# Layernorm with a residual add: the first store moved ahead of two loads in the transfer queue

## The chip, the cores and the metric

The kernel runs on one core of one Trainium2 chip. The metric is the device time of one execution in microseconds (us), the median of several. The span on a profile page is about 1.3 us shorter than that time. Engines are named as the profile names them: DVE is VectorE, ACT is ScalarE, POOL is GpSimd, and SP is SyncE, which here computes nothing and only issues transfers.

## The reference

```python
z = x + residual                      # 16 x 1024 x 512, float32
mean = np.mean(z, axis=-1, keepdims=True)
var = np.var(z, axis=-1, keepdims=True)
out = gamma * (z - mean) / np.sqrt(var + eps) + beta
```

Two inputs of 33.55 MB are read and one output of 33.55 MB is written, 100.66 MB in all. Each input byte is used once.

## The kernel before

The kernel calls 128 tokens (one per partition, 2 KiB each) a row. There are 128 rows. Sixteen rows of one tensor are 4 MiB. All large transfers are issued by SP, in the order of a written plan; `x0+8` loads rows 0 to 7 of x, `r` is the residual, `o` the store of finished rows.

```python
Z_ROWS = 64      # rows of zbuf: x comes here, is added to, normalized, and stored from here
R_ROWS = 32      # rows of rbuf: the residual

PLAN = """
x0+8 r0+8 x8+8 r8+8 x16+16 r16+16 x32+16 r32+16
x48+16 r48+16 o0+16 r64+16 x64+16 o16+16 r80+16 x80+16
o32+16 r96+16 x96+8 x104+8 o48+16 r112+16 x112+8 x120+8
o64+16 o80+16 o96+16 o112+12 o124+4
"""
ADDS = [4, 4, 8] * 7 + [4] * 4        # rows per POOL instruction
```

SP walks this plan. A wait in front of one transfer also holds everything behind it in the plan:

```python
for kind, lo, n in moves:
    if kind == "x":      # the rows of zbuf must have been stored
        while gone < len(stores) and stores[gone][0] < lo + n - Z_ROWS:
            nc.sync.wait_ge(so[gone], 16)
            gone += 1
        move(...)
    elif kind == "r":    # the rows of rbuf must have been added
        wait_rows(s_add, "add", lo + n - R_ROWS)
        move(...)
    else:                # the rows must be finished
        wait_rows(s_out, "out", lo + n)
        move(...)
```

So x48 waits for nothing, r48 waits until rows 0 to 31 are added, r64 until rows 0 to 47 are, x64 until o0 has landed, and o0 until DVE has finished rows 0 to 15. On the other engines, POOL adds r to x in zbuf (L180), ACT makes the sums over each row in groups of four rows (L202 and L212), and DVE normalizes the same groups (L240 and L252).

## Time and profile before

| | before |
|---|---|
| time, median of 3 runs | 238.39 us |
| span in the profile | 236.9 us |
| load/store queue, share of 16 engines' span | 99.2% |
| ACT, DVE, POOL busy | 78%, 75%, 60% |

These are lines of the page of the kernel before. The row DMA is the busy share of the 16 DMA engines in 40 slices of 5.9 us, in tenths; the row below it is what they moved; "q1" is the queue of all large transfers.

```profile
span 236.9 us, 1471 instructions
PE 3.7 (2%) x4; PEld 1.2 (0%) x4; DVE 177.2 (75%) x290; ACT 185.5 (78%) x545; POOL 143.0 (60%) x29
DMA  8999999999999999999999999999999999999996
GB/s 310 443 432 426 426 443 443 443 443 443 426 415 398 443 443 443 426 420 409 431 437 443 443 443 432 420 407 429 443 437 437 409 432 448 437 420 437 426 430 285
q1 hardware_dynamic: 4176, 100.67, 99.2%
```

No slice but the first and the last falls below 9, and the mean is 425 GB/s.

The timeline of SP in the kernel before, from 31 to 99 us. The columns are the start, the duration of the issue instruction, the engine and line, the operation, and out<-in. By the plan, the lines are r32, x48, r48, o0, r64, x64, o16, r80.

```profile
31.01 0.33 SPq L146 DMA_DIRECT2D rbuf<-in_residual_dram  x1
31.38 0.43 SPq L146 DMA_DIRECT2D zbuf<-in_x_dram  x1
59.41 0.33 SPq L146 DMA_DIRECT2D rbuf<-in_residual_dram  x1
59.78 0.43 SPq L146 DMA_DIRECT2D out_dram<-zbuf  x1
78.83 0.33 SPq L146 DMA_DIRECT2D rbuf<-in_residual_dram  x1
90.61 0.33 SPq L146 DMA_DIRECT2D zbuf<-in_x_dram  x1
90.98 0.43 SPq L146 DMA_DIRECT2D out_dram<-zbuf  x1
98.55 0.33 SPq L146 DMA_DIRECT2D rbuf<-in_residual_dram  x1
```

The timeline of POOL in the kernel before: the adds of rows 32 to 47, 48 to 63 and 64 to 79. In brackets is the idle time before, and what ended it.

```profile
60.98 17.83 POOL L180 TENSOR_TENSOR zbuf<-zbuf,rbuf 128x2048 f32<-128x2048 f32 x3 [1.60 <-DMA rbuf<-in_residual_dram]
80.67 17.84 POOL L180 TENSOR_TENSOR zbuf<-zbuf,rbuf 128x2048 f32<-128x2048 f32 x3 [1.87 <-DMA rbuf<-in_residual_dram]
109.81 17.85 POOL L180 TENSOR_TENSOR zbuf<-zbuf,rbuf 128x2048 f32<-128x2048 f32 x3 [11.29 <-DMA zbuf<-in_x_dram]
```

The start of an add says when its last load landed: r32 at 60.9 us, r48 at 80.7, x64 at 109.8. The transfers thus land in plan order, 4 MiB each 9.7 to 9.9 us. When SP issued r48 at 59.41 us, r32 was just ending and x48 was still to come.

### The profile page before, as it was taken

The numbers are of one execution on the slowest core, as the hardware profiler recorded it, in microseconds if no ns is written. First come the engines' busy times: TensorE is split into PE (matmuls) and PEld (weight loads), VectorE is DVE, ScalarE is ACT, GpSimd is POOL, SyncE is SP. The second block draws the span as 40 slices with busy tenths as digits, with TensorE's granted clock in tenths as the row PEclk, the third lists the DMA queues.
The fourth block names the chain that finished last, engine by engine and source line by source line (L and its number), as shares of the span: only waits on it lengthen the run. The fifth ranks groups of instructions, "written<-read, shape, count | busy, mean of one in ns | idle before, by whom it ended". The sixth has DMA issues, their size and how long they took to land.

```text
span 236.9 us, 1471 instructions
## 1 busy us (share of the span) xinstructions
PE 3.7 (2%) x4; PEld 1.2 (0%) x4; DVE 177.2 (75%) x290; ACT 185.5 (78%) x545; POOL 143.0 (60%) x29
## 2 busy tenths in 40 slices
PE   0600000000000000000000000000000000000000
PEld 0100000000000000000000000000000000000000
DVE  0001977939699999999898989896989895698920
ACT  2019879497999999999999998979998956999300
POOL 0098920999799699604995059944995049950000
DMA  8999999999999999999999999999999999999996
GB/s 310 443 432 426 426 443 443 443 443 443 426 415 398 443 443 443 426 420 409 431 437 443 443 443 432 420 407 429 443 437 437 409 432 448 437 420 437 426 430 285
DMA packets 4181, 100.68 MB, mean 425 GB/s; under 512 B 466, under 2 KB 466, under 8 KB 468
## 3 DMA queue, kind: packets, MB, share of 16 engines
q1 hardware_dynamic: 4176, 100.67, 99.2%
q14 instruction: 1, 0.01, 0.0%
q10 hardware_dynamic: 4, 0.00, 0.0%
HBM read 67.11 MB, written 33.55 MB: 425 GB/s over the span
## 4 chain that ended last, share of the span: by engine, by line
DMA 71%; POOL 9%; ACT 9%; DVE 2%; issue 2%; SPq 1%; ACTq 0%; DVEq 0%; POOLq 0%
DMA out_dram<-zbuf 49%; DMA rbuf<-in_residual_dram 16%; POOL zbuf L180 9%; DMA zbuf<-in_x_dram 6%; ACT junk_s L212 5%; ACT junk_m L202 4%; SPq L146 1%; DVE zbuf L240 1%; DVE zbuf L252 1%; ACTq L202 0%; DVEq L240 0%; ACT std L221 0%; DVE rstd L249 0%; ACTq L193 0%; POOLq L177 0%
## 5 line engine op out<-in xcount | busy, mean ns | idle before, releaser
L180 POOL TENSOR_TENSOR zbuf<-zbuf,rbuf 128x2048 f32<-128x2048 f32 (+1 forms) x25 | 142.8, 5740 | 67.6 <-DMA zbuf<-in_x_dram 40.8
L240 DVE SCALAR_TENSOR_TENSOR zbuf<-zbuf,nm,gamma_p 128x512 f32 x128 | 87.1, 743 | 46.3 <-ACT junk_s L212 46.3
L202 ACT ACTIVATE junk_m<-zbuf 128x512 f32 x128 | 74.9, 585 | 29.1 <-POOL zbuf L180 27.5
L212 ACT ACTIVATE junk_s<-zbuf,nm 128x512 f32 x128 | 88.8, 694 | 1.0
L252 DVE SCALAR_TENSOR_TENSOR zbuf<-zbuf,rstd,beta_p 128x512 f32 x128 | 87.1, 743 | 1.1
L212 ACT ACTIVATION_READ_ACCUMULATOR junk_s<-zbuf,nm 128x1 f32 x128 | 23.9, 187 | 0.0
L202 ACT ACTIVATION_READ_ACCUMULATOR junk_m<-zbuf 128x1 f32 x128 | 23.9, 187 | 0.0
L221 ACT ACTIVATE std<-ssq,eps_t 128x4 f32<-128x4 f32 x32 | 9.5, 297 | 3.0
L249 DVE RECIPROCAL rstd<-std 128x4 f32<-128x4 f32 x32 | 5.5, 170 | 0.0
L190 ACT ACT_TABLE_LOAD x1 | 1.3, 1283 | 2.7 <-PEq L60 2.7
L132 PE MATMUL gamma_p<-gb_row,ones 1*128 1x512 f32 x2 | 2.0, 1119 | 7.2 <-DMA gb_row<-in_gamma_dram 7.2
L132 PE MATMUL beta_p<-gb_row,ones 1*128 1x512 f32 x2 | 1.9, 1052 | 0.0
L127 DVE MEMSET ones<- 1x128 f32 x1 | 0.2, 165 | 2.0 <-PEq L60 2.0
L132 PEld LDWEIGHTS beta_p<-gb_row,ones 1*128 1x128 f32 x2 | 0.7, 328 | 1.0 <-issue 0.5
L132 PEld LDWEIGHTS gamma_p<-gb_row,ones 1*128 1x128 f32 x2 | 0.5, 308 | 7.1 <-issue 7.1
L288 POOL MEMSET const-float32-0.0<- 128x1 f32 x1 | 0.1, 98 | 0.2 <-issue 0.2
L288 POOL MEMSET const-bfloat16-1.0<- 128x1 bf16 x1 | 0.1, 101 | 0.0
L288 POOL MEMSET const-uint8-127<- 128x1 uint8 x1 | 0.1, 101 | 0.0
L288 POOL MEMSET const-float32-1.0<- 128x1 f32 x1 | 0.1, 98 | 0.0
L128 DVE MEMSET eps_t<- 128x1 f32 x1 | 0.1, 59 | 0.0
## 6 DMA issues: line engine op xcount, KB each, us to landing
rbuf<-in_residual_dram SPq DMA_DIRECT2D x7, 4096.0 KB, 30.5
out_dram<-zbuf SPq DMA_DIRECT2D x7, 4096.0 KB, 28.6
zbuf<-in_x_dram SPq DMA_DIRECT2D x5, 4096.0 KB, 28.9
zbuf<-in_x_dram SPq DMA_DIRECT2D x6, 2048.0 KB, 14.9
rbuf<-in_residual_dram SPq DMA_DIRECT2D x2, 2048.0 KB, 15.7
out_dram<-zbuf SPq DMA_DIRECT2D x1, 3072.0 KB, 13.5
out_dram<-zbuf SPq DMA_DIRECT2D x1, 1024.0 KB, 10.2
gb_row<-in_gamma_dram ACTq DMA_DIRECT2D x1, 2.0 KB
```

What stands on the lines that cost most here:

```text
L127: nc.vector.memset(ones[:, :], 1.0).then_inc(s_const, 1)
L132: nc.tensor.matmul(dest[:, :], ones[:, :], gb_row[:, k * D : (k + 1) * D], start=True, stop=True).then_inc(s_pe, 1)
L146: i = nc.sync.dma_start(out=out, in_=in_).then_inc(s, 16)
L180: nc.gpsimd.tensor_tensor(out=z, in0=z, in1=part(rbuf, R_ROWS, lo, n), op=ALU.add).then_inc(s_add, n)
L190: act.preload_act_table_set("sqrt_and_others")
L202: i = act.activation(out=junk_m[k][:, :], in_=zk[k], func=ACT.Identity, scale=-inv_d, accum_out=nm[j][:, k : k + 1],)
L212: i = act.activation(out=junk_s[k][:, :], in_=zk[k], func=ACT.Square, bias=nm[j][:, k : k + 1], accum_out=ssq[j][:, k : k + 1],)
L221: act.activation(out=std[j][:, :], in_=ssq[j][:, :], func=ACT.Sqrt, bias=eps_t[:, 0:1], scale=inv_d,).then_inc(s_std, TURN)
L240: dve.scalar_tensor_tensor(out=zk[k], in0=zk[k], scalar=nm[j][:, k : k + 1], in1=gamma_p[:, :], op0=ALU.add, op1=ALU.mult,)
L249: dve.reciprocal(out=rstd[j][:, :], in_=std[j][:, :]).then_inc(s_dve, TURN)
L252: i = dve.scalar_tensor_tensor(out=zk[k], in0=zk[k], scalar=rstd[j][:, k : k + 1], in1=beta_p[:, :], op0=ALU.mult, op1=ALU.add,)
L288: nc = _bacc.Bacc("TRN2", target_bir_lowering=False, num_devices=1)
```

## The change

The store of the first 16 rows is queued ahead of the two loads of the fourth 16 rows instead of behind them. The intent that the diff suggests: the store's place in zbuf comes free earlier, so that x64, which goes there, can be issued earlier.

```diff
-x48+16 r48+16 o0+16 r64+16 x64+16 o16+16 r80+16 x80+16
+o0+16 x48+16 r48+16 r64+16 x64+16 o16+16 r80+16 x80+16
```

## The prediction

> **What bounds the kernel.** The transfers. The page's queue line puts the load/store queue at 99.2% of 16 engines' span; the slice row for DMA reads 9 in every slice but the first and last; 10-us windows from 2 to 227 us show a DMA share of at least 0.95. 100.68 MB at the mean of 425 GB/s is the span, 236.9 us. The Trainium skill, "DMA: Bandwidth & Descriptors", section "Measured", has the same 425 GB/s for a 16 MB load on one core alone, so no spare rate is left. ACT has 78%, DVE 75%, POOL 60%.
>
> **What changes.** Only the SyncE queue's order: from x48, r48, o0 to o0, x48, r48. Before, the timeline shows x48 issued at 31.4 us, r48 at 59.4 (after the adds of rows 16 to 31), o0 at 59.8. Now x48 stands behind o0's wait for 16 finished rows. DVE finishes row 15 at 48.3 us, so o0 goes out then and x48 at about 48.7.
>
> **Does the queue run dry?** No. The skill's same page, "Queues, rings and completion order", says each DMA engine takes descriptors in ring order; the trace agrees (r32 lands at 60.9, r48 at 80.7, o0 at 90.6; about 9.8 us per 4 MiB). At 48.3 us the ring still holds 12.6 us of work. Then, estimated at 9.8 us each: o0 lands at 70.7, x48 at 80.5, r48 at 90.4. From there the order is the old one: r64 (issued at 78.8 as before), x64, o16, landing near 100, 110, 120. The early o0 lets x64 and o16 be issued at about 79 instead of 91, but behind the same bytes, so neither lands earlier.
>
> **The cost.** Rows 48 to 63 are complete at 90.4 instead of 80.7, so POOL adds them at 90.4 to 108.2 (it was idle for 11.3 us before 109.8). ACT is on rows 32 to 47 until about 95 and then needs row 48; the first 4 rows are added at 94.9. The 8-row add ends at 108.2, ACT wants it near 106.7: an estimated 1.6 us of delay. DVE's gaps of 0.93 and 1.95 us near 149 and 162 take it up. r80 goes out at 108.2 instead of 98.6, with 11 us still in the ring. In the tail, the last stores need rows finished at 220.9 and 226.6; those follow from x loads landing near 192.8, which don't move.
>
> So about 0 us lies on the critical path: a DMA-bound schedule with its bytes permuted. Prediction 238.4 us, range 237.6 to 239.4; faster by over 2% 0.01, within 2% 0.96, slower by over 2% 0.03.
>
> **What the profile would show.** Right: o0 issued near 48.3, x48 48.7, r48 59.4; POOL's fourth full 16-row group at about 90, the fifth still at about 109.8; SyncE not waiting 12 us for o0 to land; DMA at 9 in every middle slice. Wrong: a DMA slice below 9 near 50 to 60 or 108 us; POOL's fifth group well after 109.8; r80 or o48 past their old turn.
>
> **What would make it wrong.** A store placed earlier among loads moves at another rate (I read none: 434 GB/s in 81 to 90.6 us, o0's turn, beside 433 in 42 to 52); the ring holds fewer transfers than I assume; or ACT's delay does not fade and reaches the tail, where about 6 us of queued stores would still hide it (estimate from the last two stores' 13.5 and 10.2 us from issue to landing).

## The result, and the profile after

The changed kernel took 238.49 us (median of 6 runs, 238.44 to 238.70), the kernel before 238.48 us (6 runs, 238.26 to 239.47). The ratio is 0.9997, with a 95% interval of 0.9979 to 1.0014. A ratio is the mean time of one kernel's runs over that of the other's in the same rounds, so it isn't quite the ratio of the medians quoted.

The same lines of the page of the changed kernel:

```profile
span 237.1 us, 1471 instructions
DMA  8999999999899999999999999999999999999997
GB/s 310 440 428 437 426 437 442 442 442 442 354 442 442 442 437 431 420 420 426 431 442 442 437 431 426 409 426 428 450 442 426 406 423 448 437 442 426 437 413 301
q1 hardware_dynamic: 4176, 100.67, 99.2%
```

The queue's share is the same 99.2%. One slice, from 59 to 65 us, reads 8 and 354 GB/s; it is taken up below.

The timeline of SP in the changed kernel, in windows from 31 to 109 us: r32, o0, x48, then r48, r64, x64, o16, r80. In the fifth line two issues, r48 and r64, are merged; asked for 70 to 85 us alone, the timeline puts r64 at 79.54 us.

```profile
31.05 0.33 SPq L146 DMA_DIRECT2D rbuf<-in_residual_dram  x1
48.35 0.35 SPq L146 DMA_DIRECT2D out_dram<-zbuf  x1
48.74 0.43 SPq L146 DMA_DIRECT2D zbuf<-in_x_dram  x1
59.44 20.43 SPq L146 DMA_DIRECT2D rbuf<-in_residual_dram  x2
79.91 0.43 SPq L146 DMA_DIRECT2D zbuf<-in_x_dram  x1
80.39 0.43 SPq L146 DMA_DIRECT2D out_dram<-zbuf  x1
108.70 0.33 SPq L146 DMA_DIRECT2D rbuf<-in_residual_dram  x1
```

x48 was issued 17.4 us later than before (48.74 against 31.38), because it stood behind the store's wait. x64 and o16 were issued more than 10 us earlier (79.91 against 90.61). Both differences are large, and neither reached the end of the kernel. The timeline of POOL in the changed kernel, with the same three adds, shows why:

```profile
61.67 17.84 POOL L180 TENSOR_TENSOR zbuf<-zbuf,rbuf 128x2048 f32<-128x2048 f32 x3 [2.26 <-DMA rbuf<-in_residual_dram]
90.82 17.86 POOL L180 TENSOR_TENSOR zbuf<-zbuf,rbuf 128x2048 f32<-128x2048 f32 x3 [11.31 <-DMA rbuf<-in_residual_dram]
110.22 17.85 POOL L180 TENSOR_TENSOR zbuf<-zbuf,rbuf 128x2048 f32<-128x2048 f32 x3 [1.55 <-DMA zbuf<-in_x_dram]
```

The fourth 16 rows were added 10.15 us later (90.82 against 80.67), the fifth only 0.41 us later. POOL's idle time of 11 us moved from behind the fourth group to in front of it. Here is the one new wait that this made on ACT, a line of ACT's timeline in the changed kernel:

```profile
108.90 0.60 ACT L202 ACTIVATE junk_m<-zbuf 128x512 f32 x1 [1.56 <-POOL zbuf L180]
```

In the kernel before, ACT's pause at that place (107.47 us) was 0.20 us. The waits of SP, summed by what ended them, show the same exchange. First the kernel before, then the changed one; the columns are us in total, times, longest us:

```profile
SPq L146 <- DMA out_dram<-zbuf: 74.0, 4, 21.0
SPq L146 <- DVE zbuf L252: 46.0, 3, 22.0
```

```profile
SPq L146 <- DVE zbuf L252: 62.9, 4, 21.8
SPq L146 <- DMA out_dram<-zbuf: 52.6, 3, 20.9
```

SP lost one wait for a landing store (21.4 us less in sum) and won one wait for DVE (16.9 us more). Neither is time of the kernel, since the engines had work all the while.

### The profile page after: what moved, and what is told of

It is laid out like the page before. It is cut to its first block, busy times and chain, and to the rows that moved or that the text cites. A ratio compares the mean times of both kernels' runs of the same rounds, so it can differ in the third digit from the quotient of the medians.

```text
span 237.1 us, 1471 instructions
## 1 busy us (share of the span) xinstructions
PE 3.7 (2%) x4; PEld 1.2 (0%) x4; DVE 177.2 (75%) x290; ACT 185.5 (78%) x545; POOL 143.0 (60%) x29
## 3 DMA queue, kind: packets, MB, share of 16 engines
q1 hardware_dynamic: 4176, 100.67, 99.2%
## 4 chain that ended last, share of the span: by engine, by line
DMA 68%; POOL 13%; ACT 9%; DVE 2%; issue 2%; SPq 1%; ACTq 0%; DVEq 0%; POOLq 0%
DMA out_dram<-zbuf 41%; DMA rbuf<-in_residual_dram 21%; POOL zbuf L180 13%; DMA zbuf<-in_x_dram 6%; ACT junk_s L212 5%; ACT junk_m L202 4%; SPq L146 1%; DVE zbuf L240 1%; DVE zbuf L252 1%; ACTq L202 0%; DVEq L240 0%; ACT std L221 0%; POOLq L177 0%; DVE rstd L249 0%; ACTq L193 0%
```

## The experiments

Two theories can explain an unchanged time.

- Theory A: the time is set by the transfers alone. As long as the ring, the queue of issued transfers, never runs dry, any order gives the same time; later rows only use up idle time of POOL, ACT and DVE.
- Theory B: there was a gain (x64 and o16 issued earlier) and a loss (rows 48 to 63 later, an ACT stall of 1.56 us), and the two cancelled.

Ten kernels were run. The table is for orientation; each is told below. "Plan" names the place of the first store, where nothing else is said.

| label | plan | us, this | us, before in the same rounds | ratio, 95% interval |
|---|---|---|---|---|
| e1_fine_adds | changed kernel, finer adds | 238.44 | 238.29 | 1.0014, 1.0001 to 1.0028 |
| e10_half | between x48 and r48 | 238.36 | 238.17 | 1.0008, 0.9995 to 1.0022 |
| e9_swap_64 | changed kernel, x64 ahead of r64 | 238.36 | 238.17 | 1.0007, 0.9993 to 1.0021 |
| e2_before_r32 | ahead of r32 | 241.04 | 238.29 | 1.0118, 1.0102 to 1.0133 |
| e7_x64_first | ahead of r32, and x64 ahead of r64 | 239.61 | 238.31 | 1.0055, 1.0039 to 1.0071 |
| e4_mid_x32 | between two halves of x32 | 244.34 | 238.29 | 1.0256, 1.0241 to 1.0272 |
| e3_before_x32 | ahead of x32 | 249.23 | 238.29 | 1.0458, 1.0442 to 1.0474 |
| e5_after_r64 | behind r64 | 243.38 | 238.44 | 1.0209, 1.0192 to 1.0227 |
| e6_tail | o64 ahead of the last x loads | 244.06 | 238.44 | 1.0230, 1.0214 to 1.0245 |
| e8_switches | alternating halves | 238.49 | 238.31 | 1.0006, 0.9992 to 1.0020 |

### e1_fine_adds: take the loss away

```diff
 # against the changed kernel
-ADDS = [4, 4, 8] * 7 + [4] * 4
+ADDS = [4, 4, 8] * 3 + [4] * 4 + [4, 4, 8] * 3 + [4] * 4
```

> The changed order, with the fourth 16 rows added in four steps of 4 rows instead of 4, 4 and 8: takes away the ACT stall of 1.56 us that the changed order brought near 108 us. Theory A (the queue of transfers never runs dry and that alone sets the time): the stall falls below 0.4 us and the time stays, 238.5 us within 0.4. Theory B (a gain from the earlier store and a loss from the later rows cancel): without the loss the gain shows, about 1.5 us, 237.0 us.

ACT's timeline shows the stall gone. The line at the same place reads:

```profile
107.50 0.60 ACT L202 ACTIVATE junk_m<-zbuf 128x512 f32 x1 [0.20 <-issue]
```

The time was 238.44 us, against the 238.49 us of the changed kernel and 238.29 us of the kernel before in these rounds. No gain appeared. Theory B's 237.0 us is ruled out: there was no hidden gain for the stall to cancel.

### e3_before_x32 and e4_mid_x32: make the ring run dry

```diff
 # e3, against the changed kernel
-x0+8 r0+8 x8+8 r8+8 x16+16 r16+16 x32+16 r32+16
-o0+16 x48+16 r48+16 r64+16 x64+16 ...
+x0+8 r0+8 x8+8 r8+8 x16+16 r16+16 o0+16 x32+16
+r32+16 x48+16 r48+16 r64+16 x64+16 ...
 # e4: ... r16+16 x32+8 o0+16 / x40+8 r32+16 x48+16 ...
```

> The first store two transfers further ahead than in the changed kernel, before both loads of the third 16 rows. Theory A: the ring is empty from the landing of r16 (41.5 us) until the store issued at 48.35 moves its first bytes, about 1.5 to 2 us later; the gap of 8 to 9 us goes whole into the time: 246.5 to 247.5 us, with DMA slices clearly below 9 near 42 to 50 us. Theory B: order by itself costs little; the time grows by the compute delay alone, and the idle DMA time is partly won back later: below 244 us.

> Between the last two: the first store between two halves of the x32 load. Theory A: the first half keeps the ring filled until about 46.4 us, so the gap is 3.5 to 4 us: 242 to 242.5 us. If gaps in the transfers are partly won back later: below 240.5 us.

e3 took 249.23 us, 10.9 us more than the kernel before; e4 took 244.34 us, 6.1 us more. Both lie above what theory A gave, by 1.7 us or more, so its numbers were missed; what its rival gave was missed by far more. The DMA rows of the page of e3 show the hole, from 41 to 49 us:

```profile
DMA  8999994199999999899999999999999999999996
GB/s 320 436 428 428 444 455 196 85 423 338 423 428 444 455 449 386 375 423 423 418 428 423 423 423 423 428 444 418 455 439 423 418 423 444 428 439 444 439 408 296
```

In the trace's records of single packets, counted from the start of the span as everything else here, e3's last packet before the hole ends at 41.00 us and the next starts at 49.28 us; in e4 the hole runs from 45.77 to 49.08 us. The holes are 8.3 and 3.3 us long, where the theory said 8 to 9 and 3.5 to 4. In both, the first packet came 0.85 us after SP had begun to issue the store (48.43 and 48.24 us), not 1.5 to 2 us as expected for e3. But 2 to 3 us of the loss lie outside the hole. They are accounted for below, in "The ledger".

### e2_before_r32 and e7_x64_first: late rows with and without a dry ring

```diff
 # e2, against the changed kernel
-x32+16 r32+16 / o0+16 x48+16 r48+16 r64+16 x64+16 o16+16
+x32+16 o0+16 / r32+16 x48+16 r48+16 r64+16 x64+16 o16+16
 # e7, against e2
-... r48+16 r64+16 x64+16 o16+16
+... r48+16 x64+16 r64+16 o16+16
```

> The first store one transfer further ahead, before the residual load of the third 16 rows. At 48.35 us the ring should still hold about 2.8 us of the x32 load. Rows 32 to 47 are complete only near 71 us instead of 61, and ACT should stall 4 to 5 us more near 71 to 75 us, three times the stall of the changed kernel. Theory A: no dry ring, so 238.5 us within 0.7. Theory B: the loss grows by 3 to 4 us while the gain grows little, 241 to 243 us.

> e2_before_r32 took 241.04 us where theory A as first stated said 238.5. Its trace says r64 was issued only when POOL had added rows 32 to 47, near 90 us, just before the ring emptied (about 1.1 us of idle engines), and that packets were slow at this and the later change from loads to stores (2.0 us more than in the kernel before). Here x64, which by then waits for nothing, goes ahead of r64, so the ring has 9.8 us more; the compute delay is the same (ACT stalls of about 5.5 and 1.5 us near 72 to 90 us stay). Theory A (the ring must not run dry): 238.4 to 239.2 us. Theory B (the compute delay itself costs): 241.0 us as before.

e2 took 241.04 us. Theory A's 238.5 us, as first stated, was a miss, and the measured time lies at the edge of what theory B had foretold. The trace points to another route than theory B's: the late rows made a transfer late. This line of e2's POOL timeline shows rows 32 to 47 added until 89.9 us:

```profile
72.09 17.81 POOL L180 TENSOR_TENSOR zbuf<-zbuf,rbuf 128x2048 f32<-128x2048 f32 x3 [12.78 <-DMA rbuf<-in_residual_dram]
```

r64, which waits for them, was issued at 89.93 us, and r48 was then down to its last packets. Packets in flight say that the equivalent of 1.1 us of all 16 engines was idle between 89.6 and 91.5 us. That hole had not been seen in the plan: the first estimate looked for it at the store, and compared issues with landings without the 0.85 us from an issue to its first packet.

e7 keeps the late rows and closes this hole by putting x64, which is free by then, into the ring ahead of r64. It took 239.61 us, 1.4 us less. The same two stalls of ACT are in both. First e2, then e7:

```profile
76.84 0.60 ACT L202 ACTIVATE junk_m<-zbuf 128x512 f32 x1 [5.54 <-POOL zbuf L180]
90.12 0.60 ACT L202 ACTIVATE junk_m<-zbuf 128x512 f32 x1 [1.52 <-POOL zbuf L180]
```

```profile
76.50 0.60 ACT L202 ACTIVATE junk_m<-zbuf 128x512 f32 x1 [5.15 <-POOL zbuf L180]
89.78 0.60 ACT L202 ACTIVATE junk_m<-zbuf 128x512 f32 x1 [1.52 <-POOL zbuf L180]
```

So two stalls of 6.7 us in sum are in a kernel that is only 1.3 us slower than the kernel before; theory B's 241.0 us for e7 is ruled out. But theory A's upper limit of 239.2 us was missed too, by 0.4 us. The 1.3 us were lost before the last loads landed: the last block's adds start at 194.30 us instead of 192.86, and POOL had waited 11.52 us for those loads, so the computation at the end did not lose them.

```profile
194.30 17.97 POOL L180 TENSOR_TENSOR zbuf<-zbuf,rbuf 128x2048 f32<-128x2048 f32 x4 [11.52 <-DMA zbuf<-in_x_dram]
```

What they are made of is in the ledger.

### e5_after_r64: the other direction

```diff
 # against the kernel before
-x48+16 r48+16 o0+16 r64+16 x64+16
+x48+16 r48+16 r64+16 o0+16 x64+16
```

> The other direction: the first store one load later than in the kernel before, behind r64, so that x64, which waits for the store to land, finds nothing else in the ring. Theory A: a gap of 1.5 to 3 us at about 100 us (landing, the semaphore, the issue, the first bytes), 240 to 241.5 us. If the place of the store doesn't matter in itself as long as the bytes are the same: 238.5 us within 0.5.

It took 243.38 us, 4.9 us more, where theory A gave at most 241.5 us. There were two holes, not one. The expected one, at x64, ran from 101.38 us to 102.70 us. The other was at 80 us, the equivalent of 0.5 us of all engines: r64 waits for the adds of rows 32 to 47, which end at 78.8 us, the store stood behind it, and so nothing was left when r48 landed at 80.4 us. More than half of the loss, 2.9 us, is slow packets (see the ledger). SP's timeline, with r48 and r64 merged in the first line, then o0 and x64:

```profile
59.39 19.79 SPq L146 DMA_DIRECT2D rbuf<-in_residual_dram  x2
79.22 0.43 SPq L146 DMA_DIRECT2D out_dram<-zbuf  x1
101.74 0.33 SPq L146 DMA_DIRECT2D zbuf<-in_x_dram  x1
```

Here the store of the kernel before had been the filling. This is the part that the intent of the change had right: a store that stands too late does cost, but in the kernel before it didn't stand too late.

### e6_tail: the same swap where no work is left to hide it

```diff
 # against the kernel before
-o32+16 r96+16 x96+8 x104+8 o48+16 r112+16 x112+8 x120+8
-o64+16 o80+16 o96+16 o112+12 o124+4
+o32+16 r96+16 x96+8 x104+8 o48+16 r112+16 o64+16 x112+8 x120+8
+o80+16 o96+16 o112+12 o124+4
```

> The same kind of swap in the last block: the store of rows 64 to 79 goes ahead of the last x loads instead of behind them, in the kernel before. No gap opens at the swap, but the last rows are complete 9.8 us later and nothing but stores remains to hide it. Theory A with the tail slack read as about 6 us: the ring runs dry near 222 us, waits for the rows of the last two stores, and the time grows by 3 to 6 us: 241.5 to 244.5 us. If the tail hides 10 us or more: 238.5 us within 0.5.

It took 244.06 us, 5.6 us more. A line of POOL's timeline shows the last block 10.3 us late (192.86 us in the kernel before), and the page's DMA row shows the hole near the end:

```profile
203.12 17.94 POOL L180 TENSOR_TENSOR zbuf<-zbuf,rbuf 128x2048 f32<-128x2048 f32 x4 [21.73 <-DMA zbuf<-in_x_dram]
```

```profile
DMA  8999999999999999999999999999999999999197
```

So the tail hides 10.3 - 5.6 = 4.7 us of delay, less than the estimate of 6 us in the prediction. The time from an issue to its first packet, which that estimate left out, is part of the difference: 0.83 us here (231.12 to 231.95 us). The engines were all idle from 227.5 to 231.95 us, later than the 222 us expected.

### e8_switches: does alternating loads and stores cost?

```diff
 # against the kernel before
-x48+16 r48+16 o0+16 r64+16 x64+16 o16+16 r80+16 x80+16
+x48+16 r48+16 o0+8 r64+8 o8+8 r72+8 x64+16 o16+8 r80+8 o24+8 r88+8 x80+16
```

> The kernel before with the first two stores and the residual loads of rows 64 to 95 cut into halves and alternated: eight changes between loading and storing where there were four, no wait made longer than the ring covers. If stores among loads move at the loads' rate and a change costs nothing while the ring is full: 238.4 us within 0.7. If each change costs as much as those in e2 to e5 (0.5 to 0.9 us each): 240.5 to 242 us.

It took 238.49 us, a ratio of 1.0006. Alternation in itself costs nothing measurable while the ring is full: 0.20% at most by the interval.

### e9_swap_64 and e10_half: is it the residual load next to the store?

```diff
 # e9, against the changed kernel
-o0+16 x48+16 r48+16 r64+16 x64+16
+o0+16 x48+16 r48+16 x64+16 r64+16
 # e10, against the kernel before
-x48+16 r48+16 o0+16
+x48+16 o0+16 r48+16
```

> The changed kernel with x64 ahead of r64 (as in e7, but without e7's late rows 32 to 47). In e7 the last packets of r64, just before the store o16, took 0.85 us too long in sum, and in the changed kernel the last packets of x64 before o16 took no excess. If it is the residual load next to a store that is slow: about 0.85 us more than the changed kernel, 239.3 us. If e7's excess came with its late compute or its late issue of r64 and o16: 238.5 us within 0.4.

> The half step: the store between x48 and r48. Rows 48 to 63 are complete as late as in the changed kernel, near 90.5 us, the store lands 10 us later than there. Theory A: the ring never runs dry, 238.5 us within 0.5, as both kernels. If the residual load next to the first store is what costs 0.4 to 0.6 us in both kernels, an x load next to it is free: 238.0 us, with next to no slow packets at the store.

Both took 238.36 us (238.17 us for the kernel before in these rounds). In e9, r64 in front of o16 had no slow packets, and in e10, x48 in front of the first store had 0.4 us of them. The idea that the residual load is at fault fell. As a half step of the change, e10 also agrees with theory A: both kernels and the step between them take the same time.

### The ledger

The trace records each packet of a transfer with its start, its duration and its size. Outside a few places, a packet of 32 KiB takes 1.213 to 1.222 us. Two sums were made for each profiled run, over the data packets of queue q1. "Idle" is the time that the 16 engines had no packet in flight, divided by 16. "Slow" is what packets took beyond 1.216 us per 32 KiB, where that is over 60 ns, divided by 16. The next table gives each sum less that of the kernel before (2.86 us of idle, nearly all in the first 2 and last 5 us, and 1.10 us of slow, most of it in the first 5 us), and beside their total the difference of the spans.

```
run             idle   slow   total   span, measured difference
after          -0.06   0.18    0.12    0.21
e1_fine_adds    0.05  -0.03    0.02    0.05
e2_before_r32   0.99   2.00    2.99    2.90
e3_before_x32   9.05   2.12   11.17   11.04
e4_mid_x32      3.63   2.12    5.75    5.75
e5_after_r64    2.12   2.92    5.05    4.94
e6_tail         5.68   0.12    5.80    5.96
e7_x64_first    0.00   1.34    1.33    1.12
e8_switches     0.04   0.27    0.31    0.50
e9_swap_64     -0.03   0.16    0.13    0.10
e10_half        0.07   0.02    0.09    0.06
```

The two sums give every span difference within 0.25 us. They nearly have to: all runs move the same bytes through the same 16 engines, so whatever lengthens a run shows as idle engines or as slow packets, a wait for computation too (the holes of e2 and e6 are such waits). The ledger thus says where time went and does not by itself choose between the theories. The choice rests on the runs: e1, e9 and e10 changed waits and order, and the time by no more than 0.3%; e7 has no more idle than the kernel before in spite of its stalls; and e3 and e4 lost more than the length of their holes. What the ledger adds to theory A is a second way to lose time, slow packets.

They come in a few places. Every run has 0.4 to 0.7 us of them in its first 5 us. The runs without a hole before loads have some at the change to the first store and, e7 apart, little at later changes: 0.37 us in the kernel before, at 77 to 80 us, 0.62 us in the changed one, at 57 to 61 us, and 0.17 to 0.63 us in e1, e6, e8, e9 and e10, with at most 0.16 us at any later place. The runs with a hole before loads (e2 to e5; in e3 and e4 it is a second, small one at r64, of 0.5 and 0.4 us) have 0.5 to 0.8 us where the loads start again and 0.9 to 1.1 us at the next change from loads to a store. In e2, e3, e4 and e7 there are 0.8 to 0.9 us of them around the end of the first store, from 58 us on. e7, without any hole in the middle, has 0.85 us more at the change from r64 to o16, so its whole loss is slow packets. Why the packets are slow there, and not at the same change in e9, stays open: e7 differs from e9 in its late rows 32 to 47 and in its late issue of r64 and o16, and no run separates the two.

No version beat both kernels. There is little to win: in the kernel before, the engines have less than 0.1 us of idle time between 2 and 232 us.

## Why the prediction was right

- **What bounds the kernel**: right. The queue's share stayed at 99.2%, and taking away the ACT stall (e1) changed nothing. The Trainium skill, "DMA: Bandwidth & Descriptors", section "Measured", states 425 GB/s for a 16 MB load (there issued from GpSimd); this kernel, loads and stores issued from SyncE, has the same 425 GB/s.
- **The issues**: o0 and x48 were predicted at 48.3 and 48.7 us and came at 48.35 and 48.74. r48, predicted at 59.4, came at 59.44. The same page says, in "Anatomy of one DMA" (a section on transfers issued from GpSimd), that DMA engines do not wait on semaphores and that any wait happens on the issuing sequencer; x48, which waits for nothing, standing 17.4 us behind the store's wait is that sentence in this trace.
- **The ring does not run dry**: right, and e4 and e3 show what happens when it does: 3.3 and 8.3 us of hole cost 6.1 and 10.9 us. The changed kernel kept 12.6 us in hand at the store by the landing of r32 at 60.9 us (61.67 us in fact); counted to first packets it is 0.85 us less. In this plan the store could not go one whole load further ahead without loss, as e2 shows.
- **The later rows**: predicted for 90.4 us, they came at 90.82; the ACT stall, predicted at 1.6 us, was 1.56 us. Taking it away (e1) changed nothing. It faded as predicted: near 162 us DVE's gap fell from 1.95 us to 1.33 us, and the last block's adds start 0.21 us later.
- **What the earlier store bought**: nothing, as predicted. x64 was issued 10.7 us earlier and landed 0.4 us later, since it stood behind the same bytes.
- **What was off**: one of the signs that were to show it wrong came, faintly: a DMA slice of 8, from 59 to 65 us. Its 354 GB/s is 88 GB/s below its neighbour's 442, which is one round of 16 packets of 32 KiB in a slice of 5.9 us, so part of the 8 is only where that round falls. The rest is the change to the first store, whose slow packets sum to 0.62 us (0.37 us in the kernel before, at its own place). The prediction knew no such cost, and read "no difference" from rates over 10 us. That the cost stayed this small was luck as far as the prediction goes: one load further ahead (e2, e7) the slow packets took 1.3 to 2.0 us more than in the kernel before. In the changed kernel the slow packets moved r32's landing by 0.7 us; at the end of the span 0.2 us were left, and in the time nothing that could be measured. The tail's slack was put at 6 us; e6 measured 4.7.

## What to carry to other kernels

When the transfers are busy from end to end, ask of a reordering only two things: does the backlog of issued transfers outlast the longest wait it puts in front of the others, counted from the issue to the first packet, and do the rows that now come later feed an engine that has idle time before the end. Where both held, the reordering was free and useless in the changed kernel, e8, e9 and e10; in e7 both held too, and slow packets whose cause is open still cost 0.55%, so the two questions are not quite the whole test. The same store two loads further ahead cost 4.6%, and the same kind of swap in the last block 2.3%. Follow the delay also into the next waits: the holes that were missed in e2 and e5 were not at the moved store but at r64, whose issue hung on the rows that came later, or on what no longer stood in front of it.

## What the Trainium skill lacked or had wrong

- "DMA: Bandwidth & Descriptors", section "Specifications", gives about 0.6 us as the first-byte latency of transfers issued from SyncE and doesn't say from when it counts. With an empty ring, the first packet started 0.85 us after the start of the issue instruction in e3 and e4 (a store), 0.96 us in e5 (x64) and 1.01 us at the start of the kernel before (x0). The issue instruction itself lasts 0.33 to 0.38 us; counted from its end it is 0.5 to 0.6 us, so the page's figure fits if it counts from there.
- The same page doesn't say how many bytes may wait in a ring. In the kernel before, SP had issued 20 MiB by 4.3 us, with none of the issues taking over 0.5 us, so nearly that much fits at least (about 0.9 MB had moved by then).
- No page tells of the slow packets: 0.37 to 0.62 us in sum at the first store among loads in the two kernels, and 0.5 to 0.8 us where loads start again after a dry ring, with 0.9 to 1.1 us at the next store (e2 to e5), while later changes between loads and stores cost 0.06 us or less with a full ring (e8).
